# Output projection of a hybrid encoder layer: the second half of the tokens tile by tile, with all of w_out split and held

## The chip, the cores and the metric

One core of one Trainium2 chip runs the whole layer. The metric is the device time of one execution in microseconds (us). The engines are TensorE (PE, with its weight loads as PEld), VectorE (DVE), ScalarE (ACT), GpSimd (POOL) and SyncE (SP); DMAs are issued from the queues of SP and ACT. Each engine runs its instructions in the order of its own queue.

## The reference

One layer on 1024 tokens of width 1024, in float32. Three branches (an S5 state space model, a short convolution, and forgetting attention) read one input projection; they are merged by gates, projected, and added to x under a norm; then comes a squared-ReLU MLP. What the change touches is the middle:

```python
merged = (gates[:, :, 0] * jnp.einsum('blc,cd->bld', y_a, wa)
          + gates[:, :, 1] * jnp.einsum('blc,cd->bld', y_b, wb)
          + gates[:, :, 2] * jnp.einsum('blc,cd->bld', y_c, wc))
mix = jnp.einsum('bld,de->ble', merged, w_out)
x = x + rmsnorm(mix, g_post_mix)
h = rmsnorm(x, g_pre_mlp)
ff = jnp.einsum('blf,fd->bld', jnp.square(jax.nn.relu(jnp.einsum('bld,df->blf', h, w_ff1))), w_ff2)
return x + rmsnorm(ff, g_post_mlp)
```

## The kernel before

Every large product is made three times: both operands are split into a high and a low part (`split`, L72 to L77: ACT copies the high part, DVE subtracts to get the low part), and TensorE sums high·high, high·low and low·high. A weight block is therefore loaded by SP into a buffer of the tag `raw` (two buffers, 1 MB each at most), then split into buffers of the tags `wH` and `wL` (three each) or of the tag `e8` (six, pool `ext`).

The order of the program is set by a hand-made clock. `mm` adds the modelled time of each matmul to `clk`; generators put on a heap by `spawn` are continued by `poll` as soon as `clk` has passed the time that they yielded. `settle` runs everything that is on the heap to its end. From this program a planner of the framework sets the final order on each engine.

The tokens go in two halves of 512 (th 0 and 1), the eight tiles of 128 tokens are t = 0 to 7. The stages around the change, in order:

- the S5 branch, in four quarters (`s5_quarter`), each a chain of small products between DVE and ACT steps, filled with input projections. The last product of a quarter, `pz`, is emitted 6.5 clock units after the gelu steps whose result `gq` it reads (L792).
- attention, then the merge. `merge_item` (th, dp, b) multiplies branch b with its rows of w_branch for two of the eight output tiles (24 matmuls), DVE multiplies by the gate, POOL sums. After the third branch `merged` splits the sum into `mT`, the operand of the output projection. The first four items (half 0, branch 0, `mga`) still use the old PSUM pool, tag `pj`, two banks; later ones use the pool `mp` (`mps`, eight banks).
- `wo0`: output projection of half 0, four weight blocks (kc, e), each over tiles 0 to 3 (`rows_item`). With the last block `mix(t)` is spawned, 10 units apart.
- `mg1`: the twelve merge items of half 1, beside the mixes of tiles 0 to 3.
- `wo1`: output projection of half 1. Blocks (0,0) and (0,1) over tiles 4 to 7, then `wo_last`: for each tile the blocks (1,0) and (1,1), and after each tile `mix(t)`. Only the last two blocks are held split together.
- `mix(t)` is a chain for one token tile: ACT squares and sums (`rms_scale`), POOL works out the reciprocal root in eight small steps, DVE scales, POOL (half 0) or DVE (half 1) adds x, ACT squares again and issues the store of the row, POOL again, DVE scales into `hr`, TensorE transposes `hr` (`pth`, eight transposes), and ACT and DVE make the MLP's operands from it. In half 1 these are sums and differences for a Strassen-like scheme, split into ten tiles `tk` (T1 to T4 and B22). `hr` also takes the unused output of both squares; in half 1 it has two buffers, and is taken at the start of the chain.
- `ff1_early`: the products P1 and P2 of eight pairs of the MLP (12 matmuls each), which need half 0 only. The mixes of half 1 run beside them. Then `ff1_stages`, whose first product P6 needs `tk` of all four tiles of half 1.

## Time and profile before

| | us |
|---|---|
| median of 3 runs | 1678.66 |
| lowest, highest | 1673.03, 1679.43 |
| the profiled execution | 1678.55 |
| its span in the trace | 1676.8 |
| TensorE busy in the span | 1613.7 |

The span is what the profiler saw of the program, 1.75 us less than the profiled execution's device time. A matmul's recorded length overlaps with the next one's, so the step from one start to the next is what a matmul costs. The idle time in brackets in a row is what the engine sat still before that instruction, with the instruction that released it.

### The profile page before, as it was taken

The numbers are of one execution on the slowest core, as the hardware profiler recorded it, in microseconds if no ns is written. First come the engines' busy times: TensorE is split into PE (matmuls) and PEld (weight loads), VectorE is DVE, ScalarE is ACT, GpSimd is POOL, SyncE is SP. The second block draws the span as 40 slices with busy tenths as digits, with TensorE's granted clock in tenths as the row PEclk, the third lists the DMA queues.
The fourth block names the chain that finished last, engine by engine and source line by source line (L and its number), as shares of the span: only waits on it lengthen the run. The fifth ranks groups of instructions, "written<-read, shape, count | busy, mean of one in ns | idle before, by whom it ended". The sixth has DMA issues, their size and how long they took to land.

```text
span 1676.8 us, 20962 instructions
## 1 busy us (share of the span) xinstructions
PE 1613.7 (96%) x7783; PEld 1331.5 (79%) x7783; DVE 1024.1 (61%) x1511; ACT 703.4 (42%) x1060; POOL 514.8 (31%) x610
## 2 busy tenths in 40 slices
PE   7999999999999999999899899799999999999997
PEld 6787888889888787877787677688878878888886
DVE  4868657433264563777573654968887674545665
ACT  5322223231354453565334335644444454443442
POOL 1087654000422214120143633444443300101132
PEclk9999999999999999999999999799999999999999
DMA  5421332430653526242773465246645599755521
GB/s 163 123 67 55 82 101 88 125 105 9 213 186 139 196 79 223 84 156 98 255 244 108 168 226 152 88 144 206 195 151 167 170 343 367 253 190 197 180 97 51
DMA packets 186034, 261.73 MB, mean 156 GB/s; under 512 B 24752, under 2 KB 108764, under 8 KB 183884
## 3 DMA queue, kind: packets, MB, share of 16 engines
q1 hardware_dynamic: 170380, 228.93, 42.4%
q10 hardware_dynamic: 15552, 31.46, 5.0%
q8 instruction: 61, 1.00, 0.2%
q14 instruction: 41, 0.34, 0.1%
HBM read 183.54 MB, written 75.63 MB: 155 GB/s over the span
## 4 chain that ended last, share of the span: by engine, by line
PE 43%; DVE 7%; issue 4%; POOL 3%; ACT 2%; DMA 2%; SPq 0%; DVEq 0%; ACTq 0%; POOLq 0%
PE P L122 13%; PE P4f L122 3%; PE P3f L122 3%; PE P6f L122 3%; PE P5f L122 3%; PE P2f L122 3%; PE P7f L122 3%; PE P1f L122 2%; PE p_g L122 2%; PE pb L122 1%; PE wo101p L122 1%; PE wo100p L122 1%; PE ps L122 1%; PE p_q L122 1%; PE av L122 1%
## 5 line engine op out<-in xcount | busy, mean ns | idle before, releaser
L65 DVE TENSOR_TENSOR st<-x,st 128x1024 fp32r<-128x1024 f32 x70 | 86.7, 1250 | 77.9 <-ACT st L73 77.9
L122 PE MATMUL p_g<-hT,w_g_0H 128*128 128x512 f32 x384 | 124.5, 403 | 1.2 <-ACT K L1005 1.2
L122 PE MATMUL p_g<-hT,w_g_1H 128*128 128x512 f32 x384 | 125.6, 402 | 0.0
L73 ACT ACTIVATE st<-x 128x1024 fp32r<-128x1024 f32 x70 | 73.6, 1059 | 99.0 <-PE P6f L122 16.6
L65 POOL TENSOR_TENSOR w2s<-w2s 128x512 f32<-128x512 f32 x32 | 41.8, 1307 | 223.2 <-DMA w2s<-in_w_ff 215.8
L65 POOL TENSOR_TENSOR s<-w1r 128x512 f32<-128x512 f32 x32 | 53.3, 1684 | 152.5 <-DMA w1r<-in_w_ff 131.0
L122 PE MATMUL pb<-yH,wb_0L 128*128 128x512 f32 x192 | 77.1, 401 | 10.3 <-DVE wb_0L L65 10.3
L65 DVE TENSOR_TENSOR sl<-x,sh 128x1024 fp32r<-128x1024 f32 x42 | 56.6, 1352 | 47.4 <-ACT sh L73 47.4
L122 PE MATMUL pb<-yH,wb_0H 128*128 128x512 f32 x192 | 77.0, 401 | 4.8 <-DVE macc L68 4.8
L65 POOL TENSOR_TENSOR fa<-fa,gfin 128x512 f32<-128x512 f32 x16 | 25.5, 1605 | 178.3 <-ACT fjk L1707 178.3
L122 PEld LDWEIGHTS p_g<-hT,w_g_0H 128*128 128x128 f32 x384 | 69.3, 190 | 13.0 <-ACT K L1005 1.6
L122 PEld LDWEIGHTS p_g<-hT,w_g_1H 128*128 128x128 f32 x384 | 69.6, 189 | 11.7 <-issue 0.2
L122 PE MATMUL p_g<-hT,w_g_0L 128*128 128x512 f32 x192 | 76.1, 396 | 0.0
L122 PE MATMUL pb<-yL,wb_0H 128*128 128x512 f32 x192 | 76.1, 396 | 0.0
L122 PE MATMUL p_g<-hT,w_g_1L 128*128 128x512 f32 x192 | 76.0, 396 | 0.0
L65 DVE TENSOR_TENSOR PT<-pt,PT 128x512 fp32r<-128x512 f32 (+2 forms) x96 | 53.0, 552 | 23.4 <-ACT PT L73 22.8
L73 ACT ACTIVATE sh<-x 128x1024 fp32r<-128x1024 f32 x42 | 44.2, 1057 | 51.4 <-PE P3f L122 9.9
L73 ACT ACTIVATE PT<-pt 128x512 fp32r<-128x512 f32 (+2 forms) x96 | 46.9, 489 | 41.2 <-PE pt L126 39.6
L65 POOL TENSOR_TENSOR macc<-macc,gl 128x512 f32<-128x512 f32 x16 | 28.5, 1792 | 103.2 <-DVE gl L68 103.2
L1042 ACT ACTIVATE P<-ps,mx 128x128 f32<-128x128 f32 (+3 forms) x64 | 47.3, 739 | 30.2 <-DVE mx L1039 30.1
L1039 DVE TENSOR_REDUCE mx<-ps 128x1 f32<-128x128 f32 (+3 forms) x64 | 48.1, 752 | 13.1 <-PE ps L122 12.7
L848 ACT ACTIVATE g<-p_g,bgcol 128x512 f32<-128x512 f32 x48 | 32.8, 683 | 53.4 <-PE p_g L122 53.2
(822 smaller groups left out, 4648.6 us busy)
## 6 DMA issues: line engine op xcount, KB each, us to landing
w2s<-in_w_ff SPq DMA_DIRECT2D x16, 1024.0 KB
w1r<-in_w_ff SPq DMA_DIRECT2D x16, 1024.0 KB
as<-sa SPq DMA_DIRECT2D x16, 1024.0 KB
x<-as SPq DMA_DIRECT2D x32, 512.0 KB
x<-t_P SPq DMA_DIRECT2D x32, 512.0 KB
r_g<-in_w_in SPq DMA_DIRECT2D x12, 1024.0 KB
gt_s<-g ACTq DMA_DIRECT2D x48, 256.0 KB
t_P<-w2s SPq DMA_DIRECT2D x48, 256.0 KB
```

The costliest lines, as they stand in the source:

```text
L65: (eng or dve).tensor_tensor(o, x, y, op=op)
L73: act.activation(hi, src, AF.Copy, scale=scale)
L122: pe.matmul(o, l, r, start=start, stop=stop)
L848: act.activation(g, ps, AF.Tanh, bias=bgcol[:, i:i + 1], scale=0.5)
L1039: dve.tensor_reduce(mx, sv, axis=mybir.AxisListType.XY, op=MAX, negate=True)
L1042: act.activation(Pm[:, 0:kend].rearrange("p (c n) -> p c n", c=nch), sv, AF.Exp, bias=mx, accum_out=sm)
```

## The change

- `pz` of the first S5 quarter is emitted 10 units after the gelu instead of 6.5.
- The merge items of half 0, branch 0, with dp 2 and 3 take their PSUM banks from the tag `s` (two buffers of two banks) instead of `pj`.
- `merged` yields its 2 units itself and counts how many are open.
- The mixes of tiles 0 to 3 are spawned 17 units apart instead of 10; the `settle` after the merge is replaced by waiting for the open `merged` alone.
- `wo1` and `wo_last` are replaced by `wo_block` and `wo_second`. Four blocks of w_out are loaded and split, three into `e8`, one into `wH`/`wL`: the first after the tenth merge item of half 1, the second after the eleventh, the last two after the twelfth. Then each of the tiles 4 to 7 runs through all 48 of its matmuls, and its mix is spawned.
- In the mixes of half 1 the squares write to junk tiles of the tag `tm` (two buffers), `hr` is taken only when it is written, and the transposes of tile t are held until 8·(t−4) units after the end of `wo_second`.

```diff
@@ -789,7 +789,7 @@
             bs = slice(4 * b, 4 * b + 4)
             stt(gq[:, bs].rearrange("p g c -> p (g c)"), G1[:, bs].rearrange("p g c -> p (g c)"), 1.0,
                 py[:, bs].rearrange("p g c -> p (g c)"), ADD, MUL)
-        yield SY * 6.5
+        yield SY * (6.5 if j else 10.0)
         pz = pp.tile([P, 8, P], F, name=f"pz{j}", tag="s", bufs=2)
         for g in range(8):
             mm(pz[:, g, :], BD[:, g].rearrange("p t h -> p (t h)"), gq[:, g, :],
@@ -1234,9 +1234,13 @@
     yT, mT, h2 = {}, {}, {}
     macc = {}
 
+    open_m = [0]
+
     def merged(hi, lo, m):
+        open_m[0] += 1
+        yield 2.0
         split(hi, lo, m, scale=0.5)
-        yield 0.0
+        open_m[0] -= 1
 
     def merge_item(th, dp, b):
         def run(w):
@@ -1259,7 +1263,12 @@
                 dt_ = 2 * dp + d
                 if early:
                     gt = gp.tile([P, HALF], F, name=f"gl{th}{dt_}{b}", tag="gt", bufs=2)
-                    ps = pp.tile([P, HALF], F, name=f"pb{th}{dt_}{b}", tag="pj", bufs=2)
+                    if dp < 2:
+                        ps = pp.tile([P, HALF], F, name=f"pb{th}{dt_}{b}", tag="pj", bufs=2)
+                    else:
+                        if d == 0:
+                            ps2 = pp.tile([P, 2, HALF], F, name=f"pb{th}{dt_}{b}", tag="s", bufs=2)
+                        ps = ps2[:, d]
                 else:
                     gt = mg.tile([P, HALF], F, name=f"gl{th}{dt_}{b}", tag="gl", bufs=4)
                     ps = mps(f"pb{th}{dt_}{b}")
@@ -1317,19 +1325,29 @@
         xr_ = row(f"xr{t}")
         sp.dma_start(xr_, a["x"][t * P:(t + 1) * P, :])
         yield 1.5
-        hr = hrow[0](f"hr{t}")
-        rs = rms_scale(acc, hr, f"n1_{t}")
+        hr = jk = None
+        if not th:
+            hr = jk = row(f"hr{t}")
+        else:
+            jk = r2.tile([P, D], F, name=f"jk{t}", tag="tm", bufs=2)
+        rs = rms_scale(acc, jk, f"n1_{t}")
         yield 5.0
         stt(acc, acc, rs, mixg[0], MUL, MUL)
         tt(acc, acc, xr_, ADD, dve if th else pool)
         yield 2.5 if th else 5.0
-        rs2 = rms_scale(acc, hr, f"n2_{t}")
+        if th:
+            jk = r2.tile([P, D], F, name=f"jl{t}", tag="tm", bufs=2)
+        rs2 = rms_scale(acc, jk, f"n2_{t}")
         act.dma_start(x1_s[t], acc)
         yield 5.0
+        if th:
+            hr = r2.tile([P, D], F, name=f"hr{t}", tag="hr", bufs=2)
         stt(hr, acc, rs2, mixg[1], MUL, MUL)
         c0 = (t % 4) * P
         cs = slice(c0, c0 + P)
         yield 5.0
+        while th and not (wo_done and clk[0] >= wo_done[0] + 8.0 * (t - 4)):
+            yield 1.0
         pts = []
         for kh in range(2):
             pt = mps(f"pth{t}{kh}", (P, 4, P))
@@ -1367,45 +1385,53 @@
 
     tk = {}
     EXTK = ("B22", "T1", "T2")
-    MS = 0.0
-    WP = (5, 0)
     KC = 8
 
     def wo_item(th, kc, e):
         def lhs(t, k):
             c0 = (t % 4) * P
             return mT[0, th, kc][:, k, c0:c0 + P], mT[1, th, kc][:, k, c0:c0 + P]
-        if th and kc:
-            return wo_last(lhs) if e == 0 else None
         last = kc == 1 and e == 1
         return rows_item(f"wo{th}{kc}{e}", wo_k, 4 * kc, e, range(4 * th, 4 * th + 4), lhs,
-                         (lambda t: spawn(mix(t), 10.0 * (t % 4))) if last else None)
-
-    def wo_last(lhs):
-
-        src = wo_k[:, 4:8, :]
-
-        def run(w):
...
+                         (lambda t: spawn(mix(t), 17.0 * (t % 4))) if last else None)
+
+    def wo_block(kc, e, where):
+
+        raw = ws.tile([P, 4, HALF], F, name=f"woR{kc}{e}", tag="raw", bufs=2)
+        sp.dma_start(raw, wo_k[:, 4 * kc:4 * kc + 4, e * HALF:(e + 1) * HALF])
+        if where is None:
+            return [wsplit(raw[:, 2 * i:2 * i + 2, :], [2, HALF], f"wo{kc}{e}_{i}") for i in range(2)]
+        h, l = [where(f"wo{n}{kc}{e}", [P, 4, HALF]) for n in "HL"]
+        for i in range(2):
+            sl = slice(2 * i, 2 * i + 2)
+            split(h[:, sl, :], l[:, sl, :], raw[:, sl, :])
+        return [(h[:, 2 * i:2 * i + 2, :], l[:, 2 * i:2 * i + 2, :]) for i in range(2)]
+
+    def wo_second(W):
+
+        for t in range(4, 8):
+            cs = slice((t % 4) * P, (t % 4 + 1) * P)
+            ps = {}
+            for e, kc in (((0, 0), (1, 0), (0, 1), (1, 1)) if t == 4 else
+                          ((0, 0), (0, 1), (1, 0), (1, 1)) if t < 7 else ((1, 0), (1, 1), (0, 0), (0, 1))):
+                if kc == 0:
+                    ps[e] = mps(f"wl{t}{e}")
+                for k in range(4):
+                    wh, wl = [w[:, k % 2, :] for w in W[kc, e][k // 2]]
+                    xh, xl = mT[0, 1, kc][:, k, cs], mT[1, 1, kc][:, k, cs]
+                    mm(ps[e], xh, wh, kc == 0 and k == 0, False, 0.214)
+                    mm(ps[e], xh, wl, False, False, 0.214)
+                    mm(ps[e], xl, wh, False, kc == 1 and k == 3, 0.214)
+                if kc:
+                    act.activation(accs[t][:, e * HALF:(e + 1) * HALF], ps[e], AF.Copy)
+                    if (t, e) == (5, 0):
                         pairs[0].prep_a()
-                    yield
-        return Item("wol", src[:, :, :HALF], [4, HALF],
-                    [((FULL, slice(2 * i, 2 * i + 2), FULL), [2, HALF]) for i in range(2)], run)
+                    if e == (t < 7):
+                        spawn(mix(t))
+                poll()
+        wo_done.append(clk[0])
+
+    wo_done = []
 
 
 
@@ -1785,22 +1810,24 @@
         run_items(wo0[b:b + 1], wo0[b + 1:] + mg1)
         yT[1, b] = y_split(1, b, yraw[b])
     run_items(wo0[3:], mg1)
-    run_items(mg1, wo1)
+    W = {}
+    run_items(mg1[:10], mg1[10:])
+    W[0, 0] = wo_block(0, 0, ext8)
+    run_items(mg1[10:11], mg1[11:])
+    W[1, 0] = wo_block(1, 0, ext8)
+    run_items(mg1[11:])
+    W[0, 1] = wo_block(0, 1, None)
+    W[1, 1] = wo_block(1, 1, ext8)
+    while open_m[0]:
+        clk[0] = max(clk[0], events[0][0])
+        poll()
     mg_es.close()
-    settle()
     new_acc(range(4, 8), lt)
     r2_es = ExitStack()
     r2 = r2_es.enter_context(pool_("r2"))
-    hrow[0] = lambda name: r2.tile([P, D], F, name=name, tag="hr", bufs=2)
     pairs = [Pair(i) for i in range(NF)]
     stages = ff1_stages(pairs)
-    run_items(wo1[:1], wo1[1:])
-    woe = (ext8("woeh", [P, 4, HALF]), ext8("woel", [P, 4, HALF]))
-    raw = ws.tile([P, 4, HALF], F, name="woer", tag="raw", bufs=2)
-    sp.dma_start(raw, wo_k[:, 4:8, HALF:])
-    for k in range(2):
-        split(woe[0][:, 2 * k:2 * k + 2, :], woe[1][:, 2 * k:2 * k + 2, :], raw[:, 2 * k:2 * k + 2, :])
-    run_items(wo1[1:])
+    wo_second(W)
     AH = 2
     pairs[1].prep_a()
     for i in range(0, KC, 2):
```

## Rows read from the trace of the kernel before

**Rows 1.** Page, busy time by engine; then the chain, 1400 to 1460 us (start, us, what).

```profile
PE 1613.7 (96%) x7783; PEld 1331.5 (79%) x7783; DVE 1024.1 (61%) x1511; ACT 703.4 (42%) x1060; POOL 514.8 (31%) x610
...
1407.22 43.52 PE P2f L122 x192
```

**Rows 2.** Waits of TensorE, whole span: us in total, times, longest.

```profile
PE pth L126 <- DVE hr L68: 12.9, 2, 7.2
PE pb L122 <- DVE wb_0L L65: 10.3, 5, 4.5
```

**Rows 3.** TensorE in order of time, 1038 to 1072 us (start, us, what, [idle before]).

```profile
1038.07 1.04 PE L126 MATMUL pth<-ident,hr 128*128 128x128 f32 x8
...
1038.86 0.71 PE L122 MATMUL P<-h,wa1H 128*128 128x512 f32 x2
...
1050.30 1.97 PE L126 MATMUL pth<-ident,hr 128*128 128x128 f32 x8 [5.72 <-DVE hr L68]
...
1054.63 0.71 PE L122 MATMUL P<-h,wa2H 128*128 128x512 f32 x2
...
1066.16 1.94 PE L126 MATMUL pth<-ident,hr 128*128 128x128 f32 x8 [7.20 <-DVE hr L68]
...
1071.73 0.69 PE L122 MATMUL P<-h,wa3H 128*128 128x512 f32 x2
```

**Rows 4.** ScalarE and VectorE in order of time, 1039 to 1050 us.

```profile
1039.60 1.04 ACT L1195 ACTIVATE hr<-acc 128x1024 f32<-128x1024 f32 x1
...
1041.16 1.05 ACT L1195 ACTIVATE hr<-acc 128x1024 f32<-128x1024 f32 x1
...
1048.96 1.29 DVE L68 SCALAR_TENSOR_TENSOR hr<-acc,n_5r,gmlp 128x1024 f32<-128x1024 f32 x1 [2.59 <-POOL n_5r L62]
```

**Rows 5.** SyncE's DMA issues, ScalarE, VectorE and TensorE, 975 to 1007 us.

```profile
975.80 0.38 SPq L1208 DMA_DIRECT2D r_wo<-in_w_out  x1
...
982.90 0.38 SPq L1208 DMA_DIRECT2D r_wo<-in_w_out  x1
...
1001.22 0.38 SPq L1800 DMA_DIRECT2D woer<-in_w_out  x1
...
983.38 1.06 ACT L73 ACTIVATE wo_0H<-r_wo 128x1024 fp32r<-128x1024 f32 x1 [0.27 <-DMA r_wo<-in_w_out]
...
1006.15 2.01 ACT L73 ACTIVATE woeh<-woer 128x1024 fp32r<-128x1024 f32 x2 [4.91 <-DMA woer<-in_w_out]
...
989.24 1.22 DVE L65 TENSOR_TENSOR wo_1L<-r_wo,wo_1H 128x1024 fp32r<-128x1024 f32 x1
...
997.82 0.69 DVE L68 SCALAR_TENSOR_TENSOR m<-ma,m 128x512 fp32r<-128x512 f32 x1 [1.85 <-ACT m L73]
...
988.09 0.39 PE L122 MATMUL wo100p<-wo_0H,m 128*128 128x512 f32 x1
```

**Rows 6.** VectorE, ScalarE and TensorE in order of time, 940 to 967 us.

```profile
940.26 3.04 DVE L65 TENSOR_TENSOR wb_0L<-r_wb,wb_0H 128x1024 fp32r<-128x1024 f32 x1
...
942.26 1.06 ACT L1195 ACTIVATE hr<-acc 128x1024 f32<-128x1024 f32 x1 [5.64 <-POOL acc L65]
...
961.67 0.79 PE L122 MATMUL pb<-yH,wb_0L 128*128 128x512 f32 x1 [4.46 <-DVE wb_0L L65]
...
966.09 0.39 PE L122 MATMUL pb<-yH,wb_0H 128*128 128x512 f32 x1
```

**Rows 7.** TensorE in order of time, 159 to 875 us.

```profile
159.42 2.75 PE L122 MATMUL pz<-gq,BD 128*128 128x128 f32 x16 [3.61 <-DVE gq L68]
...
816.17 0.77 PE L122 MATMUL pb<-yH,wb_0H 128*128 128x512 f32 x1 [4.58 <-DVE macc L68]
...
874.22 0.50 PE L122 MATMUL wo001p<-wo_1L,m 128*128 128x512 f32 x1 [0.20 <-DVE wo_1L L65]
```

**Rows 8.** Window: length, busy PE, PEld, DVE, ACT, POOL, granted clock; products reading T.

```profile
1032.60:1090.00 57.40, 44.34 (x189) 36.28 (x188) 45.95 (x58) 35.55 (x61) 27.16 (x49) 0.85 0.39 121
...
L122 PE MATMUL P<-T,wb_0H x32: 389/389/389, 1098.2 to 1111.4; 128*128 128x512 f32 x32
```

20 lines of the change are left out of this document (1 added, 19 removed).

## The prediction, made before the change was run

> **What bounds the kernel now.** The first view to read is busy time by engine: TensorE works 1613.7 of 1676.8 us, 96%, far ahead of every other engine [rows 1]. So the time falls only where TensorE stands idle or runs below full clock, and the next view is the table of its waits. Two entries lead it: transposes `pth` that wait for `hr`, 12.9 us in two waits, and merge matmuls `pb` that wait for a split weight, 10.3 us in five [rows 2]. Third comes the order of time on TensorE around these waits. The transposes of tiles 5 and 6 start after 5.72 and 7.20 us of idling [rows 3]. Behind each the engine is slow for a while: eight transposes take 0.79 us (1038.07 to 1038.86) and a matmul 43.52/192 = 0.227 us [rows 1, 3] when nothing is wrong. From 1050.30 to 1054.63 there are eight transposes and six matmuls, 4.33 us in place of 0.79 + 1.36 = 2.15; from 1066.16 to 1071.73 eight and nine, 5.57 in place of 2.83. That is the lower of the clock's two levels, 1.2 instead of 2.4 GHz, and costs 2.18 + 2.74 = 4.9 us. The window of this stage has a mean granted clock of 0.85 [rows 8]. The two waits thus cost 12.9 + 4.9 = 17.8 us.
>
> Why `hr` is late stands in ScalarE's order. The first square of tile 6 writes into `hr`, which has two buffers, so it starts only at 1039.60, when the transposes of tile 4 have freed one. The second square of tile 5 is queued behind it and starts at 1041.16; POOL's root and VectorE's scaling follow, and `hr` of tile 5 starts only at 1048.96 [rows 4]. It is a buffer wait, passed on through an in-order queue.
>
> **The second half's mixes.** The change takes this out in two ways. The squares write elsewhere (`tm`), so no square waits for transposes. And a tile's mix starts every 48 matmuls, 48 × 0.227 = 10.9 us, instead of every 24, 5.4 us, while the transposes are held until 0, 8, 16 and 24 clock units after the last projection. From the end of tile 5's second square (1041.16 + 1.05) to its `hr` it took 6.8 us [rows 4]; the part before that has the same steps and an add, so the whole chain is 15 to 18 us, an estimate. Tile 4 has 32.7 us of later tiles in front of its transposes, tile 7 has nine products of 12 × 0.227 = 2.7 us, 24.5 us. All four are covered. The matmul count is unchanged. The wait goes: 17.8 us, the lower bound 10 if tile 7 or the ring `tm` (two buffers for squares and for a real operand) still holds one transpose back. I take −17.8.
>
> What is late next is the operand set T. VectorE is busy 45.95 of 57.4 us between 1032.6 and 1090.0, and the first product that reads T starts at 1098.2 [rows 8]. The same products would now end about 18 us earlier, while only four scalings and adds of tiles 5 and 6, 4 × 1.29 = 5 us of VectorE [rows 4], move forward out of this window. The window has 57.4 − 45.95 = 11.5 idle us, and 8.2 lie between 1090.0 and 1098.2: 18 − 5 − 11.5 − 8.2 is below zero by 6.7. I take 0, with 8 (all of those last 8.2) as the other end.
>
> **The start of the second half.** Before, `wo1` needs one weight block in its first 10.9 us and the four are spread over 33. Now tile 4 needs all four in 10.9 us, the blocks being first read at 0, 2.7, 5.4 and 8.2 us from the start. Loads go through two buffers `raw`. The first two are asked for at the same places as now, 975.80 and 982.90, 12.3 us and 5.2 us ahead of the start at 988.09; a load takes 983.28 − 975.80 = 7.5 us there, or 4.9 us (1001.22 to 1006.15) when less runs beside it [rows 5]. A block is two splits, ScalarE 1.06 and VectorE 1.22 us each [rows 5], some 3.5 us. The second block lands at 987.8 to 990.4, is split at +3.2 to +5.8 us from the start, and only then frees the buffer for the fourth, which lands 4.9 to 7.5 us later; with 2.3 us for its first half it is ready at +10.4 to +15.6 us. It is wanted at 8.2: a wait of 2 to 7.4 us. The third, behind the first (freed at about −1.3), is ready at +5.9 to +8.5, against 5.4. The merged operand `mT` is late too: its last split ended at 997.82 + 0.69, 10.4 us after the start [rows 5], and it is now read in the third block at 5.4 + 3 × 0.68 = 7.5 us, where before 22 us of other blocks lay in front. On SyncE the fourth load waits with rows of x and the first MLP weights behind it, wanted 10 and 40 us later. The waits overlap. [...] And the mix of tile 3, shifted by 21 units, now has its store on ScalarE's queue just here: such a store holds the queue until POOL has added, 5.64 us in one row [rows 6], and the weight splits and `mT` are queued behind. Ends: +2 (only the load) and +17 (7.4 + 5.64 + 2 × 2.2). I take +8, nearer to the load, which must come, than to the sum of all.
>
> One row tells of a further price there: a weight's low part on VectorE took 3.04 us beside POOL's add, against 1.22 [rows 5, 6]. The Trainium skill (SBUF — State Buffer, Who interferes with whom) says that a VectorE instruction with two SBUF inputs and a GpSimd instruction that reads SBUF exclude each other for the whole instruction. The trace agrees (3.04 against 1.22). By that rule each of the two low splits that meet tile 3's add would lose some 1.8 us, and the start would cost 11.6 in place of 8, an estimate; it lies inside the ends above.
>
> **The first half's mixes.** The largest of the five `pb` waits, 4.46 us at 961.67, lies where tile 3's mix runs into the end of tile 2's; the ten matmuls up to 966.09 took 4.42 us in place of 2.27, another 2.15 at the lower clock [rows 6]. With 17 units between them the two meet less, and tile 3 leaves this stage for the next (counted above). The other four, 5.8 us, belong to tiles 0, 2 and 3; tile 0 doesn't move. Ends: 0 and −12.4 (10.3 + 2.15). I take −6, little less than that one wait with its clock.
>
> **The two small edits.** `pz` waits 3.61 us [rows 7]; 3.5 units more are some 16 matmuls × 0.227 = 3.6 us of projections in between, so the wait closes and with it up to 2.15 us of clock (as behind the 4.46): −5, ends 0 and −5.8. What follows `pz` (a tanh on ScalarE, two steps on VectorE, eight stores on SyncE) moves with it in the program, but since `gq` comes when it came, hardly in real time. The merge matmul at 816.17 waits 4.58 us for `macc` [rows 7], because the bank of `pj` is released by VectorE, which has a split of a y load in front. With banks of `s` the first product of `mp` finds `pj` free, but VectorE must still split that item's weight behind the same y split, and by 874.22 TensorE waits for a split again (0.20 us there, so no slack) [rows 7]. Ends 0 and −6.7; I take −2.
>
> **Sum.** −17.8 + 0 + 8 − 6 − 5 − 2 = −22.8. From the profiled execution's own 1678.55 (its span 1676.8 and 1.75 around it), within 0.2 us of the median of the runs shown, 1678.66, that is 1655.8. The forecast's own range, with two or three of the smaller terms off, is 1646 to 1667.
>
> **Rivals.**
> - The start of the second half gives back most. All of +17 there, and nothing from the first half's mixes: 1678.55 − 17.8 + 17 − 5 − 2 = 1670.8. For it: the loads and the store above. Against: the loads at 982.90 and later need not take 7.5 us, and VectorE is less busy without the other mixes. 18%.
> - The transposes still wait. If a tile of `tm` waits for an operand's readers, a square on ScalarE waits, and with it all behind it, as `hr` does now: one of the two waits stays, 9 us. 1655.8 + 9 = 1664.8; both, 1674. For it: two buffers serve three uses per tile. Against: the first two are free as soon as ScalarE has written them. 10%, at 1669 in the middle.
> - Slower. The four loads go through one after the other, since the splits that free `raw` are queued on ScalarE and VectorE behind each other's waits: 7.5 + 3.5 = 11 us each from 975.8, the fourth ready at 975.8 + 44 − 1.2 = 1018.6 instead of 996.3, 22.3 us late, plus three falls of the clock at 2.2: 28.9 in place of 8. Then the evacuations of the last merge items sit in the same queues and the first half gains nothing, and T is late by its 8: −17.8 + 8 + 28.9 + 0 − 5 − 2 = +12, 1690.7. It decides from a fourth block that is ready more than 26 us after the start. Against: the buffers of `ext` and `wH` that the splits write are free at the ends of the last three merge items. 7%.
> - Better: the start costs 2 and the first half's waits go whole, 1655.8 − 6 − 6.4 = 1643.4. 6%.
> - The forecast itself: 59%.
>
> **Range and chances.** From 1641 to 1674 it leaves out the slower rival and the outer parts of the others, some 15 to 20 in 100. About 0.5%, 8.4 us, is what a measurement of this kernel can tell from no change: faster means below 1670.3, slower above 1687.1. Faster: 59 + 6, half of the first rival, and six of the second's ten, 80. Slower: the third, 7. Within: 13.
>
> **What would show it.** In the trace after: no wait of `pth` for `hr`, and a granted clock near 1.0 from the end of the projection to the first product of T (else the second rival); a wait of the first `wl` matmuls for a split weight or for `mT`, 4 to 8 us within the first 11 us (above 20, the third rival; none, the better case); fewer than five `pb` waits, none above 4 us; no wait of `pz`. A wait of the first product of T for VectorE would show that its backlog, put at nothing, counts. The prediction is wrong if TensorE's waits have only changed their place.

## The result, and the profile after

The changed kernel takes 1664.2 us (median; 1663.87 to 1665.91) against 1676.35 of the kernel before, run beside it: a ratio of 0.993, 95% interval 0.9906 to 0.9954. The profiled execution took 1664.18 us, its span is 1662.5. The forecast was 1655.8: the gain is 12.2 us by the medians and 14.3 us between the two profiles, where 22.8 were expected.

The page's busy time shows TensorE with the same work in a shorter span [rows 1]:

```profile
PE 1614.0 (97%) x7783; PEld 1330.7 (80%) x7783; DVE 1032.6 (62%) x1511; ACT 702.6 (42%) x1060; POOL 513.3 (31%) x610
```

The table of TensorE's waits (us in total, times, longest). The 12.9 us of `pth` [rows 2] are 2.2 now; the longest wait for `macc` was 4.58 [rows 7] and is 5.4; new are four small ones of `wl`, the second half's projection, two of which stand here:

```profile
PE pb L122 <- DVE macc L68: 5.6, 2, 5.4
PE pb L122 <- DVE wb_0L L65: 5.3, 3, 2.1
...
PE pb L122 <- ACT wb_0H L73: 2.9, 1, 2.9
PE pth L126 <- DVE hr L68: 2.2, 1, 2.2
...
PE wl L122 <- DVE wo_0L L65: 0.8, 1, 0.8
...
PE wl L122 <- ACT wo_0H L73: 0.7, 1, 0.7
```

Five points of TensorE's order cut the span into the steps of the prediction: first merge matmul, first matmul of the output projection, first of its second half, first MLP product, first product that reads T. The view that sums stretches (length, then busy PE, PEld, DVE, ACT, POOL, granted clock, DMA) has the last two stretches of the kernel before:

```profile
988.10:1032.60 44.50, 43.82 (x193) 35.95 (x192) 18.36 (x18) 16.26 (x23) 13.18 (x24) 1.00 0.45 139
1032.60:1098.20 65.60, 52.54 (x225) 43.08 (x224) 49.70 (x60) 39.99 (x67) 33.04 (x53) 0.87 0.39 125
```

and of the changed kernel:

```profile
985.40:1033.80 48.40, 45.62 (x202) 36.60 (x201) 26.32 (x24) 20.08 (x31) 17.54 (x43) 1.00 0.44 140
1033.80:1083.30 49.50, 47.30 (x225) 39.28 (x224) 41.96 (x53) 33.76 (x58) 20.77 (x32) 1.00 0.44 136
```

The projection of the second half is 3.9 us longer (44.5, 48.4), the stretch behind it 16.1 shorter (65.6, 49.5), at a clock of 1.00 in place of 0.87. Look at VectorE and POOL: VectorE does 26.3 us of work beside the projection where it did 18.4, and 42.0 in place of 49.7 after it; POOL's 33.0 us after it have become 20.8.

| stretch (us) | before | after | change | predicted |
|---|---|---|---|---|
| to the first merge matmul (`pz`) | 783.6 | 779.0 | −4.6 | −5 |
| to the output projection (PSUM banks) | 77.8 | 80.0 | +2.2 | −2 |
| to its second half (first half's mixes) | 126.7 | 126.4 | −0.3 | −6 |
| to the first MLP product (start of the second half) | 44.5 | 48.4 | +3.9 | +8 |
| to the first product of T (second half's mixes, T) | 65.6 | 49.5 | −16.1 | −17.8 + 0 |
| the rest | 578.6 | 579.2 | +0.6 | 0 |
| span | 1676.8 | 1662.5 | −14.3 | −22.8 |

How far one profile can be trusted for this: up to the start of the second half the changed kernel and two of the experiments below (buffers as before, pairs) are the same program. Their profiles give 779.0, 776.6 and 777.2 for the first row, 80.0, 79.8 and 80.5 for the second, 126.4, 124.0 and 124.0 for the third. A stretch of one profile is good to about 2.5 us, and the experiments are read by several profiles where they can be. A sum of stretches is good to less: the second half starts at 985.4, 980.4 and 981.7 us in these three. The third and the fourth row of the table hang together in this. Eight of the kernels, the changed one among them, read the weight blocks of the second half in the same order, and their fourth row goes from 48.4 to 54.0 us, 51.5 on the mean; the 48.4 of the changed kernel is the lowest. In the run with the buffers as before the second half starts 5.0 us earlier than in the changed kernel and then takes 54.0, and the first MLP product comes at 1034.4, against 1033.8 in the changed kernel and 1032.6 before. So that point is read with more trust than the two rows ahead of it.

Each experiment was run beside the kernel before, whose median lay between 1676.35 and 1678.94 us. Two kernels of different experiments can therefore compare differently by their medians and by their ratios to it, by up to 4 us, and where that matters both are given.

### The profile page after: what moved, and what is told of

It reads as the page before. It is cut to its first block, busy times and chain, and to the rows that moved or that the text cites. A ratio compares the mean times of both kernels' runs of the same rounds, so it can differ in the third digit from the quotient of the medians.

```text
span 1662.5 us, 20957 instructions
## 1 busy us (share of the span) xinstructions
PE 1614.0 (97%) x7783; PEld 1330.7 (80%) x7783; DVE 1032.6 (62%) x1511; ACT 702.6 (42%) x1060; POOL 513.3 (31%) x610
## 4 chain that ended last, share of the span: by engine, by line
PE 42%; DVE 7%; issue 4%; POOL 3%; ACT 3%; DMA 2%; SPq 0%; DVEq 0%; ACTq 0%; POOLq 0%
PE P L122 12%; PE P4f L122 3%; PE P7f L122 3%; PE P3f L122 3%; PE P6f L122 3%; PE P5f L122 3%; PE P2f L122 3%; PE P1f L122 2%; PE wl L122 2%; PE p_g L122 2%; PE pb L122 2%; DVE sa L65 1%; PE p_q L122 1%; PE av L122 1%; PE ps L122 1%
## 5 line engine op out<-in xcount | busy, mean ns | idle before, releaser
L126 PE MATMUL pt<-ident,P 128*128 128x128 f32 x288 | 49.1, 279 | 3.8 <-DVE PT L65 3.1
```

Source lines behind the costliest of these rows:

```text
L126: pe.transpose(o, i, idn)
```

## The experiments

**The three edits in the first half, against the second half's part alone.** Two kernels: the second half's part alone, which is the changed kernel with `pz`, the banks and the spacing set back, and the changed kernel with only the spacing set back.

```diff
-        yield SY * (6.5 if j else 10.0)
+        yield SY * 6.5
...
-                    if dp < 2:
+                    if dp < 4:
...
-                         (lambda t: spawn(mix(t), 17.0 * (t % 4))) if last else None)
+                         (lambda t: spawn(mix(t), 10.0 * (t % 4))) if last else None)
```

> Only the second half's part of the change: w_out held whole, token tile by token tile, the mixes of half 1; `pz`, the PSUM banks and the mixes' spacing in half 0 are as before. By the two traces `pz` gave 4.6, the banks cost 2.2 and the spacing gave 0.3 us, so the kernel comes 2.7 us above the changed one: 1667. Theory of the second half: from the first matmul of the second half of the output projection to the first product of the set T 97.9 us as in the changed kernel (110.1 before). Rival: the three small edits matter together more than the traces say, since the waits behind them move; then it is 1672 or more.

> The changed kernel with the mixes of tiles 0 to 3 spawned 10 units apart, as before, instead of 17. Theory: each mix brings its own wait (1.4, 2.1, 1.9, 2.9 us in the changed kernel), wherever it lies, and spreading only moves them: the stretch from the first matmul of the output projection to the first of its second half, 126.4 us in the changed kernel (859.0 to 985.4) and 126.7 in the one before, stays within 2 us, but tile 3's transposes (0.8 us) leave the second half; the kernel is within 2 us of the changed one. Rival, by the prediction: spreading removes the large wait where tiles 2 and 3 meet; then 10 apart brings 4.5 us of wait and some 2 us of slow clock back, and the kernel is 6 us slower, 1670.

Measured: the second half's part alone 1672.05 us, 0.9958 of before (0.9945 to 0.9971); with the spacing alone set back 1669.55, 0.9943 (0.9931 to 0.9956). So the second half's part gives 0.4%, 7 us, and the three small edits together some 5, though the two intervals touch. The first expectation was low by 5 us and its rival named the number: the small edits are worth more together than their stretches show. Of the second, neither held as put. The stretch ahead of the second half hardly differs (126.8 against 126.4), as the theory said, but the kernel is slower, by 2 us by the ratios, whose intervals overlap, by 5 by the medians and by 6.5 by the profiled spans (1669.0 and 1662.5), which comes nearer to the rival. In the traces the loss shows at the first MLP product, which comes at 1038.4; in the five profiles with 17 units and POOL's add (the changed kernel, and below `pj` again, four banks, buffers as before and pairs alone) it comes at 1032.5 to 1034.4. This is TensorE in order of time with 10 units (start, length, what, [idle before, released by]), and the same matmul in the changed kernel:

```profile
994.32 0.80 PE L122 MATMUL wl<-wo_0H,m 128*128 128x512 f32 x1 [4.63 <-ACT wo_0H L73]
```

```profile
988.91 0.50 PE L122 MATMUL wl<-wo_0H,m 128*128 128x512 f32 x1 [0.68 <-ACT wo_0H L73]
```

The block of w_out that it waits for comes at 994.3, in the changed kernel at 988.9, in the other four at 986.6 to 988.3; the first load of w_out is issued at 974.52 with 10 units and at 968.94 in the changed kernel. What the spacing bought was, above all, an earlier chain of loads.

**The PSUM banks.** One run with the edit undone, one with four banks that nothing joins.

```diff
-                    if dp < 2:
+                    if dp < 4:
```

> The changed kernel with one edit undone: all early merge items take their PSUM banks from `pj` again. Theory: the edit cost 2.2 us, because the two banks of one `s` tile are followed as one tile, so that the second bank's matmuls wait for VectorE's read of the first (5.36 us in the trace of the changed kernel, and 0.27). Without it the stretch from the first merge matmul (779.0 there) to the first matmul of the output projection (859.0) takes 77.8 us instead of 80.0, as in the kernel before, and the kernel 1662 instead of 1664.2. Rival: the edit gives its gain and something else in the stretch lost it; then undoing it makes the stretch longer, 82 us or more, and the kernel 1666 or more.

```diff
-                    else:
-                        if d == 0:
-                            ps2 = pp.tile([P, 2, HALF], F, name=f"pb{th}{dt_}{b}", tag="s", bufs=2)
-                        ps = ps2[:, d]
+                    elif dp == 2:
+                        ps = pp.tile([P, 2, HALF], F, name=f"pb{th}{dt_}{b}", tag="s", bufs=2)[:, 0]
+                    else:
+                        ps = pp.tile([P, HALF], F, name=f"pb{th}{dt_}{b}", tag=("tp", "av")[d], bufs=1)
```

> The changed kernel, but the early items with dp 2 take two separate tiles of the tag `s` (one bank of each used) and those with dp 3 the tags `tp` and `av`: four banks that nothing joins. If the joined banks are what cost 2.2 us, the waits of 5.36 and 0.27 us go and the first product in the new PSUM pool finds its bank free too: the stretch 779.0 to 859.0 shrinks from 80.0 to 73 to 77 us, the kernel comes to 1657 to 1661. Rival: VectorE's order (a split of a y load ahead of everything) is the limit; then the wait moves to a split weight behind it and the stretch stays between 77 and 80 us.

Measured: undone 1665.78 us (0.992; 0.9906 to 0.9935), four banks 1662.7 (0.9898; 0.9883 to 0.9913). The stretch from the first merge matmul to the output projection, over all profiles of this study: 77.8, 78.2, 77.8, 80.6 and 78.3 with `pj`, mean 78.5; 80.0, 80.4, 79.8, 79.9 and 80.5 with the joined banks, mean 80.1; 76.6, 77.2, 76.9 and 76.7 with four separate ones, mean 76.9. So on the mean joining costs 1.6 and separating gives 1.6 against `pj`; one of the five profiles with `pj` (80.6) lies with the joined ones, so the 1.6 of joining is less sure than the 3.2 between joined and separate banks, whose profiles don't meet. TensorE in the changed kernel, the second bank of dp 3:

```profile
809.67 0.80 PE L122 MATMUL pb<-yH,wb_0H 128*128 128x512 f32 x1 [5.36 <-DVE macc L68]
810.26 0.63 PE L122 MATMUL pb<-yL,wb_0H 128*128 128x512 f32 x1
...
815.38 0.58 PE L122 MATMUL pb<-yL,wb_0H 128*128 128x512 f32 x1
815.80 0.40 PE L122 MATMUL pb<-yH,wb_0L 128*128 128x512 f32 x1
```

VectorE just ahead of it:

```profile
805.59 2.29 DVE L65 TENSOR_TENSOR yL<-yr,yH 128x2048 fp32r<-128x2048 f32 x1 [0.56 <-ACT yH L73]
807.80 1.22 DVE L65 TENSOR_TENSOR wb_0L<-r_wb,wb_0H 128x1024 fp32r<-128x1024 f32 x1
808.93 0.68 DVE L68 SCALAR_TENSOR_TENSOR macc<-gl,pb 128x512 f32<-128x512 f32 x1
```

The matmul at 809.67 writes the second bank of a tile whose first bank VectorE reads at 808.93, and that read stands behind a split of a y load and a weight. The two banks share no data, but one tile is followed as one; TensorE has the first banks of both items and then the second banks. Behind the 5.36 us TensorE is at the lower clock level: 14 matmuls from 809.67 to 815.80 take 6.13 us, where 14 x 0.227 = 3.18 would do, another 2.9. With separate banks the wait is 2.95 and comes later, as the same view of that run shows:

```profile
813.13 0.80 PE L122 MATMUL pb<-yH,wb_0H 128*128 128x512 f32 x1 [2.95 <-DVE macc L68]
```

Both stretches came out as expected (78.2 and 76.6 in these two profiles), but the times did not (1662 and 1657 to 1661 were expected). The kernel with `pj` can't be told from the changed one. The one with four banks is faster than it by 1.5 us by the medians and 5 by the ratios, so how much of its 3.4 us came through is open; in its trace most of them are lost at the start of the second half. Four banks let the second half start at 980.7 instead of 985.4, and the first MLP product comes at 1033.1 instead of 1033.8. There the same view shows the third block again:

```profile
987.83 0.80 PE L122 MATMUL wl<-wo_0H,m 128*128 128x512 f32 x1 [4.22 <-ACT wo_0H L73]
```

**POOL's add in the first half's mixes.**

```diff
-        tt(acc, acc, xr_, ADD, dve if th else pool)
+        tt(acc, acc, xr_, ADD)
```

> The changed kernel with x added on VectorE instead of POOL in the mixes of tiles 0 to 3, nothing else. Theory: POOL's add (2.38 us) is what holds the first half's mixes: ScalarE's store of the row stands 5.2 and 5.6 us behind it, a low split beside it takes 3.02 us on VectorE instead of 1.22, and the sums of the last merge items come behind it on POOL, which holds ScalarE for 7.4 us more. On VectorE the add takes 1.22. So the waits of `pb` at 941, 967 and 976 (2.07, 1.85 and 2.88 us in the changed kernel) fall to a third, the stretch from the first matmul of the output projection to the first of its second half goes from 126.4 to 121 to 123 us, and since the loads behind it start earlier as well, the start of the second half gives no more than 1 to 2 back: 1660 to 1662. Rival: VectorE is the engine that the split weights wait for, and four adds more make it later: the waits stay, and the kernel is within 1 us of the changed one or slower.

Measured: 1663.23 us, 0.9919 (0.9905 to 0.9934). POOL, VectorE and ScalarE in order of time in the changed kernel, tile 3's mix:

```profile
963.90 2.38 POOL L65 TENSOR_TENSOR acc<-acc,xr 128x1024 f32<-128x1024 f32 x1 [1.16 <-DVE acc L68]
...
964.34 3.02 DVE L65 TENSOR_TENSOR wb_0L<-r_wb,wb_0H 128x1024 fp32r<-128x1024 f32 x1
...
966.31 1.06 ACT L1195 ACTIVATE hr<-acc 128x1024 f32<-128x1024 f32 x1 [5.22 <-POOL acc L65]
```

VectorE and ScalarE with the add on VectorE:

```profile
961.41 1.23 DVE L65 TENSOR_TENSOR acc<-acc,xr 128x1024 f32<-128x1024 f32 x1
...
962.73 1.06 ACT L1195 ACTIVATE hr<-acc 128x1024 f32<-128x1024 f32 x1 [4.47 <-DVE acc L65]
...
963.15 1.22 DVE L65 TENSOR_TENSOR wb_0L<-r_wb,wb_0H 128x1024 fp32r<-128x1024 f32 x1
```

The low part of a weight takes 1.22 us in place of 3.02, ScalarE's wait falls from 5.22 to 4.47, and the four waits of the merge [rows 6] sum to 5.4 us (0.23, 2.60, 1.98, 0.63) instead of 8.2 (1.39, 2.07, 1.85, 2.88). The stretch up to the second half is 120.4 us; with the three kernels below that also carry this edit (and separate banks) the mean is 121.1, against 124.8 without it (five profiles, 124.0 to 126.4). So the reason holds, and the difference of 3.02 and 1.22 us is the price of POOL's add beside the split. The rule that the prediction quoted from the Trainium skill (SBUF — State Buffer, Who interferes with whom) agrees with this: 3.02 beside the add, 1.22 where it is gone. But the kernel gains 1 us by the medians and 2 by the ratios, which is within the noise. The second half started at 978.4, 7.0 us earlier, and its first MLP product came 2.0 us earlier. The loads behind were expected to follow; the third was issued at 979.24, 2.6 us earlier than in the changed kernel.

**Is it the buffer of `hr`?** The prediction put the two large waits of `pth` down to a buffer. The change makes two things, other buffers and another order, so one run has the buffers alone, one the order alone (with neither the buffers nor the hold on the transposes), and one the distance between the mixes alone.

Other buffers, on the kernel before:

```diff
-        hr = hrow[0](f"hr{t}")
-        rs = rms_scale(acc, hr, f"n1_{t}")
+        hr = jk = None
+        if not th:
+            hr = jk = row(f"hr{t}")
+        else:
+            jk = r2.tile([P, D], F, name=f"jk{t}", tag="tm", bufs=2)
+        rs = rms_scale(acc, jk, f"n1_{t}")
...
-        rs2 = rms_scale(acc, hr, f"n2_{t}")
+        if th:
+            jk = r2.tile([P, D], F, name=f"jl{t}", tag="tm", bufs=2)
+        rs2 = rms_scale(acc, jk, f"n2_{t}")
...
+        if th:
+            hr = hrow[0](f"hr{t}")
         stt(hr, acc, rs2, mixg[1], MUL, MUL)
```

> The kernel before with only the buffers of the second half's mixes changed: the squares write to `tm`, and `hr` is taken when it is written. The order of w_out, the spacing and the program place of the transposes stay as before. Theory of the prediction: the two waits of `pth` (5.72 and 7.20 us with 4.9 us of slow clock, 17.8 in all) are a buffer wait, so without it most of them go although the tiles still come 5.4 us apart: the stretch from the first matmul of the second half to the first product of T falls from 110.1 to 95 to 100 us, the kernel to 1661 to 1668. Rival: with the tiles 5.4 us apart VectorE and POOL can't bring `hr` in time whatever the buffers; then the stretch stays above 104 us, the kernel above 1672, and it was the order token by token and the held transposes that gave the gain.

The order alone, on the changed kernel:

```diff
-        hr = jk = None
-        if not th:
-            hr = jk = row(f"hr{t}")
-        else:
-            jk = r2.tile([P, D], F, name=f"jk{t}", tag="tm", bufs=2)
+        hr = jk = r2.tile([P, D], F, name=f"hr{t}", tag="hr", bufs=2) if th else row(f"hr{t}")
...
-        if th:
-            jk = r2.tile([P, D], F, name=f"jl{t}", tag="tm", bufs=2)
...
-        if th:
-            hr = r2.tile([P, D], F, name=f"hr{t}", tag="hr", bufs=2)
...
-        while th and not (wo_done and clk[0] >= wo_done[0] + 8.0 * (t - 4)):
-            yield 1.0
```

> The other half of that pair: the changed kernel, token tile by token tile, with the buffers as before (the squares write into `hr`, which is taken at the start of the mix) and without the hold on the transposes, which has no place when a later square needs the buffer. Theory: tile 6's square needs tile 4's transposes, and at 10.9 us from tile to tile these are through about 19 us after tile 4's projection, before tile 6's ends at 21.8; so the order alone also takes the wait out, the stretch from the first matmul of the second half to the first product of T is 97 to 101 us (97.9 in the changed kernel), and the kernel within 3 us of the changed one. Rival: the buffer binds in this order too; then a wait of `pth` for `hr` of 5 us or more appears and the kernel is 1670 or slower.

The distance alone, on the kernel before:

```diff
-    MS = 0.0
+    MS = 5.5
```

> The kernel before with one number changed: the mixes of the second half start 5.5 units further apart, on top of the 5.4 us that the tiles are apart, so tile to tile 10.9 us as in the changed kernel; the order of w_out, the buffers and all else stay. The run with the buffers alone has shown that `hr` comes late without the buffer wait too: VectorE then waits 1.5 to 2.9 us six times for POOL's roots while the steps of several tiles stand in each engine's queue. Theory: it is the crowding of the mixes that makes the transposes wait, and spacing alone is enough: the two waits of `pth` fall from 12.9 to under 4 us, the stretch from the first matmul of the second half to the first product of T from 110.1 to 95 to 101 us, the kernel to 1664 to 1670. Rival: the mixes need the 33 us of projection beside them, which only the order token tile by token tile gives (there the first mix starts 11 us after the start of the second half, here 25); then the last tile comes too late for T, the stretch stays above 105, the kernel above 1673.

Measured: buffers alone 1682.21 us, 1.002 of before (1.001 to 1.003); order alone 1665.51, 0.9927 (0.9915 to 0.994); distance alone 1672.94, 0.996 (0.9946 to 0.9974). From the first matmul of the second half to the first product of T: 110.1 us before, 111.7, 104.8 and 105.0 in the three, 97.9 in the changed kernel. The order alone is at the time expected of it, though the stretch is longer than the 97 to 101: in that run the second half also started 5.0 us earlier and lost that to the third block again (54.0 us up to the first MLP product); from there to T it is 50.8 us, against 49.5 in the changed kernel.

So the buffer theory fell: the buffers alone make the kernel 0.2% slower. With the buffer wait gone and nothing else, `hr` still comes late. TensorE's transposes of tiles 4 to 7 in that run, in order of time:

```profile
1042.54 1.04 PE L126 MATMUL pth<-ident,hr 128*128 128x128 f32 x8
...
1051.32 1.06 PE L126 MATMUL pth<-ident,hr 128*128 128x128 f32 x8 [0.59 <-DVE hr L68]
...
1064.41 1.94 PE L126 MATMUL pth<-ident,hr 128*128 128x128 f32 x8 [2.56 <-DVE hr L68]
...
1078.78 1.97 PE L126 MATMUL pth<-ident,hr 128*128 128x128 f32 x8 [6.25 <-DVE hr L68]
```

Four of VectorE's eight scalings there, two for each tile:

```profile
1025.85 1.28 DVE L68 SCALAR_TENSOR_TENSOR acc<-acc,n_4r,gpost 128x1024 f32<-128x1024 f32 x1 [5.06 <-POOL n_4r L62]
...
1042.98 1.28 DVE L68 SCALAR_TENSOR_TENSOR acc<-acc,n_6r,gpost 128x1024 f32<-128x1024 f32 x1 [2.86 <-POOL n_6r L62]
...
1062.98 1.28 DVE L68 SCALAR_TENSOR_TENSOR hr<-acc,n_6r,gmlp 128x1024 f32<-128x1024 f32 x1 [1.47 <-POOL n_6r L62]
...
1077.44 1.28 DVE L68 SCALAR_TENSOR_TENSOR hr<-acc,n_7r,gmlp 128x1024 f32<-128x1024 f32 x1 [1.70 <-POOL n_7r L62]
```

Each scaling is held by one of POOL's roots, and while VectorE waits, what is queued behind it waits too: 1.5 to 2.9 us in each of the last six. The eight scalings run from 1025.85 to 1077.44, 51.6 us here, 52.8 in the kernel before (1021.37 to 1074.19) and 55.6 in the changed one. So the chain isn't shorter where the gain is (with the distance alone it is 63.0), but it begins earlier. In the kernel before, the first scaling comes 33.3 us after the start of the second half, and two of the eight are done before the projection ends. The first, the fifth and the last in the changed kernel, VectorE again:

```profile
1005.32 1.28 DVE L68 SCALAR_TENSOR_TENSOR acc<-acc,n_4r,gpost 128x1024 f32<-128x1024 f32 x1 [5.49 <-POOL n_4r L62]
...
1028.38 1.28 DVE L68 SCALAR_TENSOR_TENSOR acc<-acc,n_6r,gpost 128x1024 f32<-128x1024 f32 x1 [2.86 <-POOL n_6r L62]
...
1060.88 2.31 DVE L68 SCALAR_TENSOR_TENSOR hr<-acc,n_7r,gmlp 128x1024 f32<-128x1024 f32 x1 [3.13 <-POOL n_7r L62]
```

The first comes 19.9 us after the start, and five of the eight are done while the projection still runs (to 1033.8). The distance alone takes away tile 6's wait and most of tile 5's, and pays with tile 7's, which had none. TensorE's transposes of tiles 5 to 7 in that run:

```profile
1055.48 1.74 PE L126 MATMUL pth<-ident,hr 128*128 128x128 f32 x8 [2.07 <-DVE hr L68]
...
1066.24 1.03 PE L126 MATMUL pth<-ident,hr 128*128 128x128 f32 x8
...
1087.44 1.97 PE L126 MATMUL pth<-ident,hr 128*128 128x128 f32 x8 [6.52 <-DVE hr L68]
```

The rival had said above 105 us and above 1673; it is 105.0 and 1672.9. In the traces the order is what counts: with it the mixes lie under the projection, and the buffers and the hold together add no more than 1.3 us (50.8 against 49.5), in medians nothing that can be told. The time of the whole kernel doesn't separate order from distance: on the first half of before, the distance alone (0.996) gains as much as the second half's part alone (0.9958), although their stretches differ by 6 us, 105.0 and 98.8; the profile behind the 98.8 is 4 us faster than that kernel's median. So that the order is worth more than the distance stands on traces alone. The buffers together with the distance, in the old order, were not run.

**Three edits together, and what the third block costs.** The four banks and the add on VectorE as above, and the hold of tile 7:

```diff
-        while th and not (wo_done and clk[0] >= wo_done[0] + 8.0 * (t - 4)):
+        while th and not (wo_done and clk[0] >= wo_done[0] + (0.0, 8.0, 16.0, 28.0)[t - 4]):
```

> Three edits on the changed kernel: the four separate PSUM banks for the early merge items, x added on VectorE in the first half's mixes, and tile 7's transposes held until 28 instead of 24 units. In the run with the separate banks alone the second half started 4.7 us earlier in the trace than in the changed kernel, but 4.0 of them were lost to a wait for the third block of w_out (4.22 us), since its load needs the raw buffer of the first, split late. If POOL's add is what makes those splits late, the banks' gain comes through with it: second half started by 976 to 978, first matmul of the first MLP product at 1027 to 1029, the wait of 2.2 us for tile 7's `hr` gone, kernel 1653 to 1656. Rival: the third block's load has its own time and gives back whatever is gained ahead of it: a wait of 4 us or more for `wo_0H`, and 1659 to 1662.

Measured: 1660.93 us, 0.9904 (0.9891 to 0.9917): the rival. The second half starts at 976.2, as the theory said, 9.2 us earlier than in the changed kernel. The wait for tile 7's `hr` is gone (0.71 us for T in its place), and this stands at the start, TensorE in order of time:

```profile
983.80 0.79 PE L122 MATMUL wl<-wo_0H,m 128*128 128x512 f32 x1 [4.75 <-ACT wo_0H L73]
985.22 0.80 PE L122 MATMUL wl<-wo_0L,m 128*128 128x512 f32 x1 [0.62 <-DVE wo_0L L65]
```

The third block's way in that run, ScalarE, VectorE and SyncE in order of time (the first block's splits, the third load of w_out, the third block's splits):

```profile
971.07 1.99 ACT L73 ACTIVATE woH<-woR 128x1024 fp32r<-128x1024 f32 x2
...
973.00 2.35 DVE L65 TENSOR_TENSOR woL<-woR,woH 128x1024 fp32r<-128x1024 f32 x2
...
975.38 0.38 SPq L1401 DMA_DIRECT2D woR<-in_w_out  x1
...
982.69 1.06 ACT L73 ACTIVATE wo_0H<-woR 128x1024 fp32r<-128x1024 f32 x1 [3.02 <-DMA woR<-in_w_out]
...
983.78 1.38 DVE L65 TENSOR_TENSOR wo_0L<-woR,wo_0H 128x1024 fp32r<-128x1024 f32 x1 [1.11 <-ACT wo_0H L73]
```

The load is issued at 975.38, as soon as the low parts of the first block (973.00 + 2.35) have freed its raw buffer; it lands 7.3 us later, after ScalarE has waited 3.02 us for it. From the first block's split to the third's it is 11.6 us, and the first block is split only at 971.07, behind a merged operand that ScalarE waited for. An earlier start of the second half doesn't move this chain by as much.

**Pairs.** Tiles 4 and 5 through the blocks together; once with the three edits, once alone.

```diff
-        for t in range(4, 8):
-            cs = slice((t % 4) * P, (t % 4 + 1) * P)
-            ps = {}
-            for e, kc in (((0, 0), (1, 0), (0, 1), (1, 1)) if t == 4 else
-                          ((0, 0), (0, 1), (1, 0), (1, 1)) if t < 7 else ((1, 0), (1, 1), (0, 0), (0, 1))):
+        ps = {}
+        for grp in ([(t, e, kc) for kc, e, t in ((0, 0, 4), (0, 1, 4), (0, 0, 5), (0, 1, 5),
+                                                 (1, 0, 4), (1, 0, 5), (1, 1, 4), (1, 1, 5))],
+                    [(6, e, kc) for e in (0, 1) for kc in (0, 1)],
+                    [(7, e, kc) for e in (1, 0) for kc in (0, 1)]):
+            for t, e, kc in grp:
+                cs = slice((t % 4) * P, (t % 4 + 1) * P)
...
```

> The kernel of the three edits (separate PSUM banks, x added on VectorE in the first half, tile 7's transposes held longer) with one more: tiles 4 and 5 go through the second half's weight blocks together, both through the first two blocks, then both through the third, then both through the fourth; tiles 6 and 7 as in the changed kernel. Theory: the third block's load is what gives the earlier gains back, because it can start only when the first block's raw buffer is split. In the kernel of the three edits the second half starts at 976.2 and the third block's first half is ready at 983.8 to 985.2: wanted 5.4 us after the start, a wait of 4.75. In pairs it is wanted 10.9 us after the start, 987.1, the fourth at 992.5, ready at 991 to 993. So the stretch from the start to the first MLP product falls from 53.2 to 45 to 46 us, the kernel from 1660.9 to 1653 to 1655. Rival: the last merged operand (split at 989 to 990) or the mixes of tiles 4 and 5, which now come 2.7 us apart, take the place of the wait; then 48 us or more, or a wait of the first product of T of over 3 us, and 1657 or more.

> The changed kernel with only the pairing of tiles 4 and 5 in the second half. Of its 48.4 us from the first matmul of the second half to the first MLP product, 192 x 0.227 = 43.5 are matmuls and 0.8 tile 3's transposes; 2.8 are four waits for split weights, the rest slow clock. Theory: in pairs each block is wanted 5 us later, the waits go, the stretch is 44.5 to 45.5 us and the kernel 1660 to 1661.5. Rival: what is saved there is lost at the first product of T, since tile 4's mix starts 8 us later and next to tile 5's; then T comes 49 us or more after the first MLP product plus a wait, and the kernel is within 1.5 us of the changed one.

Measured: 1665.0 us with the three edits (0.9914; 0.9899 to 0.9929), 4 us slower than without the pairs; alone 1670.57 (0.9949; 0.9932 to 0.9966), 6 us slower than the changed kernel. By the ratios it is 2 and 3 us, with intervals that overlap; what is sure is that neither gained what was expected. In the traces both rivals are there, and an error in the expectation; the second rival had put its kernel within 1.5 us of the changed one. TensorE of the run with pairs alone, in order of time:

```profile
988.31 0.79 PE L122 MATMUL wl<-wo_0H,m 128*128 128x512 f32 x1 [3.70 <-ACT wo_0H L73]
...
1067.69 1.94 PE L126 MATMUL pth<-ident,hr 128*128 128x128 f32 x8 [6.35 <-DVE hr L68]
```

The wait for `wo_0H` is still there, twelve matmuls after the start. The code says why: the blocks are loaded in the order (0,0), (1,0), (0,1), (1,1) of kc and e, but tile 4 reads both halves of kc 0 first, because the merged operand of kc 1 comes last. So the block that is loaded third is read second, 2.7 us after the start, and the pairs left that alone. Loading the blocks in the order in which they are read was not run. The late `hr` of tile 7 (6.35 us, 1.94 for eight transposes that take 1.06 at the full clock) is the other rival: the mixes of tiles 4 and 5 start 2.7 us apart and later, and the chain of scalings with them.

**The first block through three tiles.** The last run gives the third block time and keeps the mixes apart.

```diff
...
+        for grp in ([(4, 0, 0), (5, 0, 0), (6, 0, 0)],
+                    [(4, 1, 0), (4, 0, 1), (4, 1, 1)], [(5, 1, 0), (5, 0, 1), (5, 1, 1)],
+                    [(6, 0, 1), (6, 1, 0), (6, 1, 1)],
+                    [(7, e, kc) for e in (1, 0) for kc in (0, 1)]):
...
```

> The kernel of the three edits (separate PSUM banks, x added on VectorE in the first half, tile 7's transposes held longer), with another order at the start of the second half: tiles 4, 5 and 6 first go through the block that is loaded first, and then tile 4, tile 5 and tile 6 each through their other three; tile 7 as in the changed kernel. What the pairs showed: the block that is loaded third is used second, 2.7 us after the start, and pairing left that as it was (3.39 and 3.70 us of wait) while it brought the mixes of tiles 4 and 5 to 2.7 us from each other and `hr` of tile 7 late by 3.65 and 6.35. Here that block is wanted 8.2 us after the start, about 984.4 if the start is at 976.2, and was ready at 983.8 to 985.2; the mixes come 8.2, 8.2 and 10.9 us apart. Theory: the waits of 4.75 and 0.62 us with the slow clock behind them go, the stretch from the start to the first MLP product falls from 53.2 to 45 to 47 us, and the 8.2 us between the mixes cost T no more than 2 us: 1653 to 1658. Rival: the last merged operand, split at 989.3 to 990.0, takes the wait's place, or the mixes at 8.2 us crowd as in pairs, with `hr` of tile 7 late by 2 us or more: 1660 to 1664.

Measured: 1657.18 us, 0.9873 of before (0.9857 to 0.9889), 7 us below the changed kernel by the medians, 10 by the ratios. The last two stretches of that run, in the view that sums them:

```profile
976.40:1023.10 46.70, 45.00 (x201) 36.80 (x200) 28.25 (x29) 21.36 (x32) 22.39 (x39) 1.00 0.52 169
1023.10:1072.90 49.80, 47.37 (x226) 39.30 (x224) 39.43 (x50) 32.08 (x54) 22.45 (x36) 1.00 0.45 137
```

The projection of the second half takes 46.7 us in place of 53.2, at a clock of 1.00, and from there to T it is 49.8 us, 2.7 more than with the three edits alone (47.1). What is left of the waits in TensorE's order:

```profile
985.24 0.50 PE L122 MATMUL wl<-wo_0H,m 128*128 128x512 f32 x1 [0.51 <-ACT wo_0H L73]
986.93 0.50 PE L122 MATMUL wl<-wo_0L,m 128*128 128x512 f32 x1 [1.19 <-DVE wo_0L L65]
...
1055.60 1.06 PE L126 MATMUL pth<-ident,hr 128*128 128x128 f32 x8 [2.43 <-DVE hr L68]
...
1074.15 0.50 PE L122 MATMUL P<-T,wb_0H 128*128 128x512 f32 x1 [0.91 <-DVE T L65]
```

1.7 us for the block instead of 5.4. The theory's time and stretch held; its 2 us for T became 2.7, and tile 7's `hr` is late by 2.43 us, a part of the rival.

## Why the prediction was right and where it was wrong

The time lies in the range and faster was the likeliest verdict, but the forecast itself is 8.4 us too low, and one cause was named wrongly. Term by term:

- **Second half's mixes, −17.8: −16.1.** The size was right: the waits went with their slow clock, tile 7 kept 2.20 us. The reason was half wrong. I read the late square of tile 6 in ScalarE's order [rows 4] as the cause, as it is the step that a buffer held. It was one link of the longer chain of eight scalings and eight roots, and freeing it alone left the kernel no faster. The second way that the prediction names, the tile's mix under the projection, did the work. The estimate of 15 to 18 us for a tile's whole chain was too short: tile 7's projection ends at 1033.8 and its `hr` is begun at 1060.88, 27 us later, more than the 24.5 us of products in front of its transposes. That is where its 2.20 us come from.
- **T late, 0: 0.** The first product of T waited for nothing in the changed kernel. The margin was thinner than the 6.7 us that the sum left: the last of T's splits on VectorE ended at 1080.88, 2.4 us before the product at 1083.3. Where the rest became faster, a wait of 0.7 to 1.1 us appeared.
- **Start of the second half, +8: +3.9 in the two profiles.** The four waits of `wl` sum to 2.8 us and none is above 0.8 (the kernel before had one, of 0.7); tile 3's transposes are 0.8, and the rest isn't attributed. Over the eight kernels that read the blocks in this order it is +3.9 to +9.5, +7 on the mean, so the 8 was a fair size and the +3.9 in part the luck of a late start. The loads were asked for at 968.94, 977.75, 981.82 and 988.34, where the sum had 975.80 and 982.90 for the first two [rows 5]; with 10 units between the mixes the first is at 974.52, so the earlier loads come with the spacing. And one premise was wrong: the blocks are not first read in the order in which they are loaded. The third, needed second, is what the start waits for: 2.60 + 1.13, 4.22 + 0.63, 3.30 + 1.72, 5.30 + 1.49 and 4.75 + 0.62 where the start came earlier than 985.4, and 4.63 + 0.56 and 2.16 + 1.68 where with 10 units start and loads both came later. What counts is the distance between that block and the start, not how fast the first half is. The price of the store at this place was read from a row that doesn't show it: the 5.64 us [rows 6] stand in front of ScalarE's second square, and the store is issued 0.01 us behind that square's start. And no run ties the falls of the clock at 2.2 us, which the +17 and the slower rival add, to a length of wait: in their place the runs show a fall behind 1.98 us and none behind 3.65 (last section), and the granted clock of this stretch is 1.00.
- **First half's mixes, −6: −0.3 in their stretch, −2 to −6 in all.** The largest wait, 4.46 us [rows 6], is gone, but each mix now carries its own (1.39, 2.07, 1.85, 2.88), 8.2 us in place of 10.3. Over several profiles the stretch is 124.8 us with 17 units and 127.1 with 10, a gain of 2.3. The step that failed was to take a wait as lying where two mixes meet; it lies with POOL's add and ScalarE's second square of each mix, wherever that is. So these waits gave 2 us and not 6; the rest of the gain, as far as the times show one, came through the earlier load of the third block, which the prediction didn't count with the spacing.
- **`pz`, −5: −4.6.** Its wait of 3.61 us [rows 7] is 0.2 now. Over all profiles the first merge matmul comes at 778.6 on the mean with 10 units (ten profiles, 776.6 to 780.5) and at 783.7 with 6.5 (four, 782.3 to 785.3): −5.1.
- **PSUM banks, −2: +2.2 in the two profiles, +1.6 over all.** This is outside the ends that I gave, 0 and −6.7: I gave the gain a size and the loss none, and did not ask whether the two banks of one tile are followed apart. They are not, as the run with separate banks shows.

Put together, the sum had the first MLP product 5 us earlier than before, and it came 1.2 later: 6.2 of the 8.5 us that the two spans miss lie ahead of it, in the first half's mixes and the banks, which the smaller loss at the start made up for only in part. Of the rivals none came. The "start gives back most" was the right worry: its mechanism, the third load behind the first block's split, is there in the traces, and sets what the start can gain.

## What to carry to other kernels

A stall ahead of a late operand is a chain, and the link that shows a buffer wait need not be the one that sets its length: count how often the chain crosses two in-order engines, and ask when its first link starts. Where a stage ends in an operand that has its own pace (a load that needs a buffer that needs a split), gains ahead of it are kept only if the operand moves too, or is wanted later: compare the order of the loads with the order of first use. And two halves of one tile are one tile to whoever tracks it: give a product of its own a tile of its own.

## What the runs showed of the hardware that I had not expected

A root on POOL, eight instructions on 128 x 1 elements, takes 3.0 us (958.52 to 961.49 in the changed kernel), and nearly all of it is VectorE's loss: in the run with pairs alone four scalings of 1.28 us in a row had 2.60, 2.60, 2.88 and 2.88 us of idling ahead of them. The same eight steps on VectorE, at the start of the changed kernel, take 2.0 us (12.44 to 14.45). Whether the roots on VectorE would shorten the chain of the mixes was not run.

The lower clock level came after some waits and not after others. TensorE ran at 0.43 us a matmul behind 5.36 us of idling (809.67) and, up to 983, behind 2.88 (976.48); behind 2.20 us at 1063.33 eight transposes took 1.06 us in the changed kernel, with a clock of 1.00 in that stretch, but behind 2.18 us they took 1.65 in the run with 10 units. The widest pair, TensorE in the run of the three edits with pairs and in the run with the add on VectorE:

```profile
1063.88 1.06 PE L126 MATMUL pth<-ident,hr 128*128 128x128 f32 x8 [3.65 <-DVE hr L68]
```

```profile
964.42 0.79 PE L122 MATMUL pb<-yH,wb_0L 128*128 128x512 f32 x1 [1.98 <-DVE wb_0L L65]
```

Behind the 3.65 us the matmuls went on at 0.23 us each; behind the 1.98 us six of them took 0.43 each, the lower level. So a shorter wait can cost more than a longer one, one more reason not to trust a single profile for 2 us.
